# A second place for the attention mask, and other places for three groups of loads and transposes, in a two-layer backbone on one Trainium2 core

## The chip, the core and the metric

The kernel runs on one core of one Trainium2 chip. Five engines work side by side: TensorE (PE) multiplies, VectorE (DVE), ScalarE (ACT) and GpSimd (POOL) do the elementwise work, and SyncE (SP) issues most of the transfers; ACT issues some too. Each engine takes its own instructions in the order written for it and waits on semaphores for the others. The metric is the device time of one execution in microseconds (us), lower being better. The kernel before took 1580.21 us (median of 3 runs, 1580.18 to 1580.25).

## The reference

What is computed is a two-layer generator trunk over 1024 latent tokens and 256 context tokens of width 1024, in fp32:

```
each layer:  x += gate * mixer(adaLN(RMSNorm(x)))
layer 0:     windowed grouped-query attention, 16 heads on 4 key heads, 64 wide,
             window of 128 keys to either side, all context keys, a sink logit
             per head, times silu(gate projection), then the output projection
layer 1:     multi-head latent attention: queries through a latent of 512,
             keys and values through a latent of 256, 32 rotated key columns,
             16 heads, all keys, times silu(gate projection), output projection
end:         RMSNorm of the latent stream
```

The mask of layer 0 says which of the 128-token blocks' keys lie within 128 tokens of a query. The rotation ("rope") multiplies pairs of columns by cosines and sines of the token's row and column.

## The kernel before, in words

**Precision.** An fp32 product is made of three reduced-precision ones. Each operand is split into a high part (line 129, a cast on ACT) and a low part (line 130, a subtraction on DVE or POOL); `mm3` then issues lines 134, 135 and 136 for high times high, low times high and high times low. An operand is ready for the first product when its cast is done, and for the second only when its subtraction is.

**Stages.** Norm and value projection run to about 75 us, and the block-by-block projections of queries, keys and gates to about 323 us. Layer 0's attention then works through 40 units to about 711 us: ten 128-token tiles in the order 2, 0, 3, 1, 4, 5, 6, 7, 8, 9, and four key heads each. A unit has scores for four heads on PE (line 619), the mask, the sink and the row maximum in one DVE pass (line 630), the exponential on ACT (line 633), transposes by 128-key chunk (line 650), the product with the values (lines 667 and 668), and a rescale on POOL. The first tile is special: its keys lie in two 256-wide parts, and each part has a DVE pass of its own. Scores use two pairs of PSUM banks, so the third head's scores need the first head's DVE passes done.

From 711 to about 890 us layer 1 begins. `norm_x` loads a tile of the updated rows (line 233) and scales it (line 235 on ACT for odd tiles). `turn_h` transposes a pair of tiles in four quarters (line 248 on PE, lines 252 and 256 on ACT, 257 on DVE), and `kv_tile` multiplies a tile by the latent key and value weights (24 matmuls 288 wide). Between the tiles lie the first products of the query latent and gate projections. These are done in six groups by Winograd's form of Strassen's scheme, with seven products of sums of quarter matrices for eight. The sums over the tokens are `t_sums` (lines 1146 to 1155). A group's weights are loaded by `fetch` (line 1172), turned into operands by `op`, and multiplied by `P` (12 matmuls of 512 columns each). `early(0)` and `early(1)` fetch and prepare the first two operands of groups 2 and 3 ahead; `first_op` does it for groups 0 and 1. The small fetches (128x4x128) go through rings of 2 KB slots named `wr`. The rest of the query work runs to about 970 us, the latent attention to about 1465 us, and the output projection to the end.

**What sets the order.** Program order and a scheduler set the order on each engine; only the latent attention's loop has an order written by hand. All ordinary loads and stores are issued by SP in a single order, so one that waits for a slot holds back all behind it. `load2` issues on ACT. On-chip memory is laid out by hand in regions (F, R) by offset in KB, so two tensors at one offset share bytes and the later one's load waits for the earlier one's last reader. The mask's bytes in R (offset 92 and up) held projection weights of the last blocks before. The slot at F 4 KB of the early ring lies in the buffer `xr0` (F 4 to 8) from which updated rows are stored. F 0 to 4 is `rows0[0]`, where earlier the cosines of layer 0 (F 0 to 4, until the last key block's rotation) and later those of layer 1 lie.

Of the kernel before, what the change touches and what calls it, by code (L numbers as in the profile page):

```python
# [27 lines left out]
Z = 0.125  # L28
# [32 lines left out]
def kernel(ctx: ExitStack, tc: tile.TileContext, t, out, dbg=None):  # L61
# [480 lines left out]
    mask = r_at(92 + Z, 640).bitcast(F32)  # L542
# [32 lines left out]
    class UnitA:  # L575


        def __init__(self, ti, g):
            self.ti, self.g = ti, g
            self.isx = ti >= 2  # L580
            self.k0, self.k1 = max(2, ti - 1), min(NT - 1, ti + 1)
            self.nloc = (self.k1 - self.k0 + 1) if self.isx else 0
            self.chunks = [0, 1] + (list(range(self.k0, self.k1 + 1)) if self.isx else [])
            self.m = len(self.chunks)
            self.nk = self.m * 128
            self.Ps = []
            self.PT = {}
# [18 lines left out]
        def score(self, h):  # L606
# [20 lines left out]
            for i, (a, b, skip) in enumerate(spans):  # L627
                to = nm if b == self.nk else self.esk[:, h : h + 1]
                mk = mask[:, a + skip : b + skip]
                nc.vector.tensor_tensor_reduce(P[:, a:b], S[:, 256 + a : 256 + b], mk, 1.0, sk, ALU.add, ALU.min, to)  # L630
                sk = to
# [135 lines left out]

    def wkv_copy():
        load(out=wkv_d, in_=w_in1[:, 512:800])

    side = {20: (wkv_copy,), 21: (rows_load, 0), 22: (rows_scale, 0), 31: (rows_load, 1), 33: (rows_scale, 1)}
# [188 lines left out]
    for gp in (1, 2):  # L960
        for bi in (8, 9):
            for c in range(2):
                if (bi, gp, c) == (8, 2, 0):
                    units[0].prep_q()
                    units[0].prep()
                    units[1].prep_q()
                if (bi, gp, c) == (9, 2, 0):
                    units[1].prep()
                    load(out=mask, in_=mask_d)
# [26 lines left out]
    for ui, u in enumerate(units):  # L996
# [11 lines left out]
        for ci in range(u.m):  # L1008
# [15 lines left out]
            next_T()  # L1024
            if ci == u.m - 1:
                if nu is None:
                    xts[1] = shp(xtr.next(), 8, 256)
                    turn_h(1, rows0, xts[1], hT1[1], ada1, range(4))
# [44 lines left out]
    wr = Ring(F, [2, 4], 512)  # L1073
# [59 lines left out]
    def kr_rope():  # L1133
        u = krF[:, 2:10, :]
        o, tmp = [f_at(34.5 + i, 8, 32) for i in range(2)]
# [220 lines left out]
    def first_op(i, n):  # L1356
        groups[i].fetch((n - 1,), 1)
        groups[i].op(n)
# [3 lines left out]
    for i, ti in enumerate(order1):  # L1362
# [9 lines left out]
        if i == 5:  # L1372
            wr = Ring(F, [30, 32, 34], 512)
# [12 lines left out]
        if i == 3:  # L1386
            load(out=cosb, in_=t["cos_b"].rearrange("p (t d) -> p t d", t=8))
            load(out=sinb, in_=t["sin_b"].rearrange("p (t d) -> p t d", t=8))
# [9 lines left out]
        if i in (7, 8):  # L1398
            first_op(0, i - 6)
            first_op(1, i - 6)  # L1400
# [8 lines left out]
    kr_rope()  # L1409
# [9 lines left out]
    for gi, ns in todo:  # L1419
# [5 lines left out]
        for i, n in enumerate(ns):  # L1425
# [6 lines left out]
            if gi == 4 and i in (1, 3):  # L1432
                latent_rms(i)
            if gi == 3 and i == 1:
# [572 lines left out]
```

## Time and profile before

| | |
|---|---|
| median of 3 runs | 1580.21 us |
| profiled execution | 1576.85 us |
| its span (first to last instruction) | 1575.0 us |
| PE busy, 0 to 323 us | 310.6 of 323 |
| PE busy, 323 to 711 us | 378.6 of 388 |
| PE busy, 711 to 784 us | 69.0 of 73 |
| PE busy, 784 to 890 us | 100.3 of 106 |
| PE busy, 890 to 1575 us | 671.3 of 685 |
| mean granted clock of PE | 0.992 of full speed |

The profiled execution lies 1.85 us above its span, and 3.36 us below the median of the runs. A matmul at half clock still counts as busy, so the granted clock has to be read beside the busy time.

### The profile page before, as it was taken

What the parts mean: (1) busy time and instruction counts of PE and PEld (TensorE: products, weight loads), DVE (VectorE), ACT (ScalarE), POOL (GpSimd) and SP (SyncE); (2) the same over time, 40 slices, a digit from 0 to 9 for tenths busy, and PEclk for the clock granted to TensorE, in tenths of its full rate; (3) what the DMA queues carried; (4) which work ended last, traced back from release to release, by engine and by line L of the source; (5) the groups of instructions that cost most, each with busy time, mean ns of one, the idle gap of its engine ahead of it and who ended that gap; (6) DMA issues with size and microseconds to landing.
All of it is one profiled execution on the core that took longest, in us unless ns stands there. A gap on an engine that the chain in (4) does not pass through costs nothing. (4 is left out here: it accounts for less than half of the span.)

```text
span 1575.0 us, 25485 instructions
## 1 busy us (share of the span) xinstructions
PE 1529.6 (97%) x9238; PEld 1147.0 (73%) x9238; DVE 999.6 (63%) x1664; ACT 769.5 (49%) x1477; POOL 779.7 (50%) x816
## 2 busy tenths in 40 slices
PE   6999999989999999998999999999999999999998
PEld 4988888866767777777878878666766766766687
DVE  3969988536555556565765744677577677567354
ACT  4423322257666676665733434555555555555321
POOL 1132212117564445553355252688688688689410
PEclk9999999999999999999999999999999999999999
DMA  9466673554343334324344576223233233244251
GB/s 326 154 198 195 192 212 118 175 165 111 98 124 90 99 91 121 94 81 161 99 132 133 169 242 194 82 72 98 61 98 100 72 91 88 61 138 113 69 168 67
DMA packets 158046, 202.90 MB, mean 129 GB/s; under 512 B 14656, under 2 KB 92480, under 8 KB 157904
## 3 DMA queue, kind: packets, MB, share of 16 engines
q1 hardware_dynamic: 152416, 193.53, 41.5%
q10 hardware_dynamic: 5504, 7.74, 1.4%
q8 instruction: 73, 1.20, 0.3%
q14 instruction: 53, 0.43, 0.1%
HBM read 151.65 MB, written 51.07 MB: 129 GB/s over the span
## 5 line engine op out<-in xcount | busy, mean ns | idle before, releaser
L134 PE MATMUL PB<-arena_r 128*128 128x512 f32 (+2 forms) x990 | 369.8, 376 | 6.5 <-ACT arena_r L129 2.9
L1652 POOL TENSOR_TENSOR arena_f<-arena_f 128x512 f32<-128x512 f32 x252 | 328.0, 1302 | 81.9 <-ACT arena_f L1644 65.0
L135 PE MATMUL PB<-arena_r 128*128 128x512 f32 (+2 forms) x958 | 352.1, 368 | 2.5 <-POOL arena_r L130 2.0
L136 PE MATMUL PB<-arena_r 128*128 128x512 f32 (+2 forms) x926 | 338.5, 366 | 0.1
L130 POOL TENSOR_TENSOR arena_r<-arena_f,arena_r 128x512 fp32r<-128x512 f32 x91 | 128.3, 1422 | 300.9 <-ACT arena_r L129 247.6
L1644 ACT ACTIVATE arena_f<-PB 128x1024 f32<-128x1024 f32 x160 | 164.2, 1027 | 108.5 <-PE PB L1638 69.8
L134 PEld LDWEIGHTS PB<-arena_r 128*128 128x128 f32 x990 | 186.9, 190 | 40.5 <-ACT arena_r L422 4.6
L1603 DVE TENSOR_REDUCE arena_f<-PB 128x1 f32<-128x1024 f32 x128 | 156.0, 1219 | 86.3 <-PE PB L1601 86.2
L135 PEld LDWEIGHTS PB<-arena_r 128*128 128x128 f32 x958 | 181.3, 189 | 30.0 <-POOL arena_r L130 2.6
L136 PEld LDWEIGHTS PB<-arena_r 128*128 128x128 f32 x926 | 175.7, 190 | 28.9 <-issue 1.7
L1638 PE MATMUL PB<-arena_r 64*128 64x512 f32 (+1 forms) x1490 | 194.3, 392 | 0.4 <-ACT arena_f L1644 0.3
L630 DVE CUSTOM_DVE_ANT_0 arena_f<-PB,arena_r,small 128x640 f32<-128x640 f32 (+2 forms) x176 | 124.4, 724 | 85.9 <-PE PB L619 77.2
L1638 PEld LDWEIGHTS PB<-arena_r 64*128 64x128 f32 (+1 forms) x1490 | 135.7, 185 | 29.1 <-ACT arena_f L1644 1.8
L1660 PE MATMUL PB<-arena_f 128*64 128x512 f32 x640 | 144.4, 597 | 0.0
L129 ACT CAST arena_r<-arena_f 128x512 fp32r<-128x512 f32 (+1 forms) x146 | 86.4, 607 | 107.2 <-PE PB L136 24.1
L633 ACT ACTIVATE arena_f<-arena_f,small 128x640 f32<-128x640 f32 (+2 forms) x160 | 118.7, 743 | 37.2 <-DVE small L630 36.3
L619 PE MATMUL PB<-arena_k,arena_r 128*128 128x256 f32 (+1 forms) x576 | 114.5, 321 | 7.5 <-DVE small L630 7.1
L619 PEld LDWEIGHTS PB<-arena_k,arena_r 128*128 128x128 f32 x576 | 82.8, 191 | 36.2 <-issue 14.9
L650 PE MATMUL PB<-ident,arena_f 128*128 128x128 f32 x672 | 104.6, 274 | 1.4 <-ACT arena_f L655 1.1
L1660 PEld LDWEIGHTS PB<-arena_f 128*64 128x64 f32 x640 | 43.1, 136 | 83.2 <-issue 79.6
L199 DVE SCALAR_TENSOR_TENSOR arena_f<-arena_f,small 128x512 f32<-128x512 f32 x126 | 98.4, 829 | 1.0
L136 PE MATMUL PB<-arena_k,arena_r 128*128 128x512 f32 (+2 forms) x274 | 97.8, 357 | 0.0
(249 smaller groups left out, 2513.6 us busy)
## 6 DMA issues: line engine op xcount, KB each, us to landing
arena_f<-ada_w SPq DMA_DIRECT2D x40, 512.0 KB, 4.4
arena_r<-q_d SPq DMA_DIRECT2D x80, 256.0 KB, 4.0
arena_r<-qn_d SPq DMA_DIRECT2D x64, 256.0 KB, 3.8
arena_r<-qr_d SPq DMA_DIRECT2D x170, 64.0 KB, 3.1
arena_f<-a_w_in SPq DMA_DIRECT2D x40, 256.0 KB, 3.1
q_d<-arena_f SPq DMA_DIRECT2D x64, 128.0 KB, 2.4
qn_d<-arena_f SPq DMA_DIRECT2D x16, 512.0 KB, 3.3
arena_f<-b_w_in SPq DMA_DIRECT2D x12, 512.0 KB, 4.0
```

The lines of the kernel that those rows point to most:

```text
L130: (lo_eng or nc.vector).tensor_sub(lo, src, hi.bitcast(F32))
L134: nc.tensor.matmul(o, ah, bh, start=first, stop=False, skip_group_check=more)
L135: nc.tensor.matmul(o, al, bh, start=False, stop=False, skip_group_check=more)
L136: nc.tensor.matmul(o, ah, bl, start=False, stop=last, skip_group_check=more)
L619: nc.tensor.matmul(S[:, at : at + n], qT[:, s, hq, :], kT[:, g, k : k + n], start=s == 0, stop=s == 1)
L630: nc.vector.tensor_tensor_reduce(P[:, a:b], S[:, 256 + a : 256 + b], mk, 1.0, sk, ALU.add, ALU.min, to)
L633: nc.scalar.activation(P, P, AF.Exp, bias=nm, scale=-1.0, accum_out=self.den[:, h : h + 1])
L1603: nc.vector.reduce_max(mx[:, 32 + b : 33 + b], flat, AX.X, negate=True)
L1638: nc.tensor.matmul(S[:, t], k[r, c : c + 128], q[r], start=j == 0, stop=j == 4)
L1644: nc.scalar.activation(E, self.S, AF.Exp)
L1652: eng.tensor_add(self.acc, self.acc, E[:, t])
L1660: nc.tensor.matmul(self.pv[p : p + 64], Vq[:, cs[t], self.h % 4, :], E[:, t], start=i == 0, stop=i == 4)
```

## The change

1. **The mask has two places.** The first, at F 0 KB, is loaded from the input by ACT's queue, during the last projections; the units of the first five tiles (20 units) read it. The second is the old place in R, loaded by SP with unit 4, and read by the other units. The old load, issued just ahead of the first scores, is gone. A copy of weights in memory is moved from unit 20 to unit 19.
2. **The next pair's turns.** `turn_h` for the pair of tiles 2 and 3 was called with the last unit's fourth chunk, all four quarters; now two quarters come with its second chunk and two with its third.
3. **Places of the first query operands.** The early ring of `early(0)` is at F 2 and F 0 instead of F 2 and F 4; the later ring has a fourth slot at F 0. The fetches of the first and second operand of groups 0 and 1 are called one tile earlier than their split, where `first_op` did both.
4. **The rotation of the keys.** The loads of layer 1's cosines and sines and the rotation `kr_rope` move into the loop over the groups, and its scratch to other bytes.

```diff
-    mask = r_at(92 + Z, 640).bitcast(F32)
+    masks = [f_at(0, 640), r_at(92 + Z, 640).bitcast(F32)]
...
+            self.mask = masks[ORDER.index(ti) > 4]
...
-                mk = mask[:, a + skip : b + skip]
+                mk = self.mask[:, a + skip : b + skip]
...
+    def mask_load():
+        load(out=masks[1], in_=mask_d)
...
-    side = {20: (wkv_copy,), 21: (rows_load, 0), ...}
+    side = {4: (mask_load,), 19: (wkv_copy,), 21: (rows_load, 0), ...}
...
                 if (bi, gp, c) == (8, 2, 0):
+                    load2(out=masks[0], in_=t["mask"])
...
                     units[1].prep()
-                    load(out=mask, in_=mask_d)
                     units[2].prep_q()
...
+            if nu is None and 0 < ci < 3:
+                if ci == 1:
+                    xts[1] = shp(xtr.next(), 8, 256)
+                turn_h(1, rows0, xts[1], hT1[1], ada1, (2 * ci - 2, 2 * ci - 1))
             if ci == u.m - 1:
-                if nu is None:
-                    xts[1] = shp(xtr.next(), 8, 256)
-                    turn_h(1, rows0, xts[1], hT1[1], ada1, range(4))
...
-    wr = Ring(F, [2, 4], 512)
+    wr = Ring(F, [2, 0], 512)
...
-        o, tmp = [f_at(34.5 + i, 8, 32) for i in range(2)]
+        o, tmp = [f_at(i, 8, 32) for i in (51, 36)]
...
-            wr = Ring(F, [30, 32, 34], 512)
+            wr = Ring(F, [30, 32, 34, 0], 512)
...
         if i in (7, 8):
-            first_op(0, i - 6)
-            first_op(1, i - 6)
+            for g in groups[0:2]:
+                g.op(i - 6)
+        if i in (6, 7):
+            for g in groups[0:2]:
+                g.fetch((i - 6,), 1)
...
+            if gi == 1 and i == 0:
+                load(out=cosb, ...)
+                load(out=sinb, ...)
+            if gi == 2 and i == 0:
+                kr_rope()
```

How the rows move at three places follows. Line numbers of the changed kernel are up to seven higher; `DMAHW` in a row's waits means a transfer queue's semaphore.

The first place is PE at the start of layer 0's attention, the first unit's scores among products of the last projection (before; four score matmuls make one head of this unit):

```order
L619 MATMUL PB<-arena_k,arena_r 128x256 [waits Activation_49]
L619 MATMUL PB<-arena_k,arena_r 128x256
L134 MATMUL PB<-arena_r 128x512
L619 MATMUL PB<-arena_k,arena_r 128x256 [waits Activation_49]
L619 MATMUL PB<-arena_k,arena_r 128x256
L135 MATMUL PB<-arena_r 128x512
```

and the same place now:

```order
L620 MATMUL PB<-arena_k,arena_r 128x256 [waits Activation_49]
L620 MATMUL PB<-arena_k,arena_r 128x256
L134 MATMUL PB<-arena_r 128x512
L620 MATMUL PB<-arena_k,arena_r 128x256 [waits Activation_49]
L620 MATMUL PB<-arena_k,arena_r 128x256
L620 MATMUL PB<-arena_k,arena_r 128x256 [waits DVE_49]
L620 MATMUL PB<-arena_k,arena_r 128x256
L620 MATMUL PB<-arena_k,arena_r 128x256 [waits DVE_49]
```

The third head's scores, which wait for DVE's pass over the first head, now follow at once; before, six products, the last row of the first list and five behind it, stood ahead of them.

The second place is SP in layer 1's first stage, around the small fetches (L1172), the store of updated rows (L719) and the loads of the next tiles (L233), before:

```order
L701 DMA arena_f<-x 128x1024 [waits DMAHW2_49,Activation_49]
L1172 DMA arena_f<-b_w_in 128x4x128 [waits DMAHW5_49,DMAHW1_49,Pool_49]
L719 DMA x_d<-arena_f 128x1024 [waits DMAHW6_49,DMAHW2_49,DVE_49]
L1172 DMA arena_f<-b_w_in 128x4x128 [waits DMAHW7_49,DMAHW6_49,Activation_49]
L233 DMA arena_f<-x_d 128x1024 [waits DMAHW0_49,PE_49]
```

and now, with the same transfers under lines 702, 1177, 720 and 233, and on to the last small fetch:

```order
L702 DMA arena_f<-x 128x1024 [waits DMAHW5_49,DMAHW1_49,Activation_49]
L1177 DMA arena_f<-b_w_in 128x4x128 [waits DMAHW2_49]
L1177 DMA arena_f<-b_w_in 128x4x128 [waits DMAHW3_49,Pool_49]
L1177 DMA arena_f<-b_w_in 128x4x128 [waits DMAHW6_49,DMAHW2_49,Pool_49]
L720 DMA x_d<-arena_f 128x1024 [waits DMAHW7_49,DMAHW1_49,DVE_49]
L233 DMA arena_f<-x_d 128x1024 [waits DMAHW0_49,PE_49]
L233 DMA arena_f<-x_d 128x1024 [waits PE_49]
L233 DMA arena_f<-x_d 128x1024 [waits DMAHW7_49,DMAHW4_49,PE_49]
L1177 DMA arena_f<-b_w_in 128x4x256 [waits DMAHW6_49,PE_49,Activation_49]
L1177 DMA arena_f<-b_w_in 128x4x256 [waits DMAHW0_49,DVE_49,PE_49]
L1177 DMA arena_f<-b_w_in 128x4x128 [waits DMAHW3_49,DMAHW1_49,Activation_49]
L1437 DMA arena_f<-cos_b 128x256 [waits DMAHW5_49,DMAHW4_49,Pool_49]
```

No small fetch stands between the store and the next tile's load any more. Behind the last row stand the sines (L1438) and then the last small fetch. Six of the eight small fetches now come ahead of the tile's load, five before.

The third place is ACT at the end of the tiles, where the operands of groups 0 and 1 are cast (L129), before:

```order
L129 CAST arena_r<-arena_f 128x512 [waits DVE_49]
L1119 DMA ckv_d<-arena_f 128x256 [waits DMAHW0_49,DVE_49]
L1219 COPY arena_f<-PB 128x512 [waits PE_49]
L129 CAST arena_r<-arena_f 128x512 [waits DVE_49]
L129 CAST arena_r<-arena_f 128x512 [waits PE_49]
L129 CAST arena_r<-arena_f 128x512 [waits DMAHW7_49,Pool_49]
```

and now:

```order
L129 CAST arena_r<-arena_f 128x512 [waits DVE_49]
L1124 DMA ckv_d<-arena_f 128x256 [waits DMAHW1_49,DVE_49]
L1224 COPY arena_f<-PB 128x512 [waits PE_49]
L129 CAST arena_r<-arena_f 128x512 [waits DVE_49]
L129 CAST arena_r<-arena_f 128x512 [waits DMAHW0_49,Pool_49]
L129 CAST arena_r<-arena_f 128x512 [waits DVE_49,PE_49]
```

The cast that waits for a transfer has moved up by one, and the operand that it casts is, going by the rings, another one: before, group 1's first; now, group 0's second.

More of the change, by code (lines that the diff above doesn't have):

```diff
@@ L766, in turn_ctx @@
             split(hT1[0][:, 0, k, :], hT1[0][:, 1, k, :], u)
+    def mask_load():
+        load(out=masks[1], in_=mask_d)
     def wkv_copy():
         load(out=wkv_d, in_=w_in1[:, 512:800])
-    side = {20: (wkv_copy,), 21: (rows_load, 0), 22: (rows_scale, 0), 31: (rows_load, 1), 33: (rows_scale, 1)}
+    side = {4: (mask_load,), 19: (wkv_copy,), 21: (rows_load, 0), 22: (rows_scale, 0), 31: (rows_load, 1), 33: (rows_scale, 1)}
     side.update({23 + 2 * q: (turn_ctx, q) for q in range(4)})
@@ L1354, in early @@
         g.op(2)
-    def first_op(i, n):
-        groups[i].fetch((n - 1,), 1)
-        groups[i].op(n)
     order1 = [2 * p + j for p in (0, 1, 3, 2, 4) for j in range(2)]
@@ L1386 @@
         if i == 3:
-            load(out=cosb, in_=t["cos_b"].rearrange("p (t d) -> p t d", t=8))
-            load(out=sinb, in_=t["sin_b"].rearrange("p (t d) -> p t d", t=8))
             t13 = t_sums(xts[1], xts[3], slice(0, 256), t4buf)
@@ L1408 @@
     next(t24)
-    kr_rope()
     for f in (t13, t24):
@@ L1433 @@
                 latent_rms(i)
+            if gi == 1 and i == 0:
+                load(out=cosb, in_=t["cos_b"].rearrange("p (t d) -> p t d", t=8))
+                load(out=sinb, in_=t["sin_b"].rearrange("p (t d) -> p t d", t=8))
+            if gi == 2 and i == 0:
+                kr_rope()
             if gi == 3 and i == 1:
```

## The prediction

> **What bounds the kernel now.** I read the page's busy shares first, then PE's list of waits, then the stretches around each wait in windows and rows.
>
> ```profile
> PE 1529.6 (97%) x9238; PEld 1147.0 (73%) x9238; DVE 999.6 (63%) x1664; ACT 769.5 (49%) x1477; POOL 779.7 (50%) x816
> ```
>
> PE is busy for 1529.6 of 1575.0 us, so the kernel is PE's work plus 45.4 us of pauses, and only what shortens PE's pauses, or the slow clock behind them, moves the end. Its waits, with columns total, times and longest:
>
> ```profile
> PE PB L619 <- DVE small L630: 7.1, 5, 4.7
> PE PB L248 <- ACT arena_f L235: 3.8, 1, 3.8
> PE PB L134 <- ACT arena_r L129: 3.2, 2, 2.9
> PE PB L1312 <- POOL arena_r L130: 2.2, 1, 2.2
> PE PB L135 <- POOL arena_r L130: 2.0, 1, 2.0
> ```
>
> The first three and the fifth lie where the change works; the fourth lies outside it. Each long one is followed by a stretch at half clock, which PE's busy share hides. I call the three places the mask's, the tile's and the operand's pause.
>
> **The mask's pause.** The cast of the last rotated key block on ACT, SP's load of the mask, DVE's first two passes, PE on either side of the pause, then windows of 2 us (span, PE and its weight loads, DVE, ACT, POOL, granted clock, share and rate of transfers):
>
> ```profile
> 281.65 1.34 ACT L129 CAST arena_k<-arena_f 64x512 fp32r<-64x512 f32 x2 [2.84 <-DVE arena_f L521]
> 322.94 0.54 SPq L969 DMA_DIRECT2D arena_r<-mask_d  x1
> 330.29 0.48 DVE L630 CUSTOM_DVE_ANT_0 arena_f<-PB,arena_r,small 128x256 f32<-128x256 f32 x1 [7.55 <-DMA arena_r<-mask_d]
> 330.70 0.48 DVE L630 CUSTOM_DVE_ANT_0 arena_f<-PB,arena_r,small 128x256 f32<-128x256 f32 x1
> 323.24 0.88 PE L619 MATMUL PB<-arena_k,arena_r 128*128 128x256 f32 x6
> 324.24 0.50 PE L619 MATMUL PB<-arena_k,arena_r 128*128 128x256 f32 x2
> 330.84 0.80 PE L619 MATMUL PB<-arena_k,arena_r 128*128 128x256 f32 x2 [4.72 <-DVE small L630]
> 330.00:332.00 2.00, 1.16 (x4) 1.06 (x5) 1.71 (x9) 0.37 (x1) 0.00 (x0) 0.50 1.09 274
> 332.00:334.00 2.00, 2.00 (x10) 1.81 (x9) 1.39 (x6) 1.24 (x5) 0.00 (x0) 0.50 1.05 212
> 334.00:336.00 2.00, 2.00 (x6) 1.61 (x6) 0.49 (x2) 1.54 (x4) 0.20 (x1) 0.50 0.45 101
> ```
>
> The load goes out when PE has read the last weights in those bytes, shares full transfer engines with the queries' loads, and lands 7 us later. PE stands for 4.72 us and then runs 1.16 + 2 + 2 = 5.16 us of busy time at half clock, which is 2.6 us of lost time. Together: 7.3 us.
>
> The change loads this mask on ACT's queue, just ahead of the cast at 281.65, some 40 us earlier, so DVE's passes can start with the first scores at 323.24. One ACT issue is added there; ACT has idle time on both sides, so I cost it at nothing. What comes next is DVE's own pace. Passes start 0.41 us apart (330.29, 330.70), and the third head's scores, now right behind the second's, need the first head's two passes. With the first pass at about 323.8 these are done by 324.6, while PE arrives at 324.24 + 0.3. I leave 0.5 us for this and count **6.8**. Bounds: 7.3 if DVE keeps up, and 4.0 if PE waits for the first unit's eight passes one by one (8 × 0.41 = 3.3). The second mask's load has a whole run of units to land in, and costs PE nothing.
>
> **The tile's pause.** SP, POOL, ACT and PE around it, then windows:
>
> ```profile
> 737.97 0.45 SPq L719 DMA_DIRECT2D x_d<-arena_f  x1
> 742.30 0.37 SPq L1172 DMA_DIRECT2D arena_f<-b_w_in  x1
> 742.76 0.46 SPq L233 DMA_DIRECT2D arena_f<-x_d  x1
> 732.80 4.68 POOL L130 TENSOR_TENSOR arena_r<-arena_f,arena_r 128x512 fp32r<-128x512 f32 x3 [6.14 <-PE PB L135]
> 745.40 0.62 ACT L129 CAST arena_r<-arena_f 128x512 fp32r<-128x512 f32 x1 [3.46 <-DMA arena_f<-b_w_in]
> 746.89 1.14 ACT L235 ACTIVATE arena_f<-arena_f,small 128x1024 f32<-128x1024 f32 x1
> 748.09 0.66 PE L248 MATMUL PB<-ident,arena_f 128*128 128x128 f32 x4 [3.79 <-ACT arena_f L235]
> 748.00:750.00 2.00, 1.91 (x12) 1.92 (x13) 1.56 (x2) 1.77 (x3) 1.52 (x1) 0.77 0.00 0
> 750.00:752.00 2.00, 2.00 (x10) 2.00 (x9) 2.00 (x3) 1.43 (x5) 0.00 (x0) 0.50 0.19 66
> 752.00:754.00 2.00, 2.00 (x15) 2.00 (x15) 1.56 (x5) 1.92 (x5) 0.99 (x1) 0.88 0.01 4
> ```
>
> The small fetch at 742.30 goes into bytes from which the store at 737.97 still reads; SP stands for it, and the tile's load goes out only behind it, at 742.76. The price is 3.8 us of pause and a clock loss of 1.91 × 0.23 + 2 × 0.50 + 2 × 0.12 = 1.7 us: 5.5 us.
>
> With the ring at F 2 and F 0 that fetch no longer waits for the store, and all early fetches stand ahead of it. One more fetch now waits for a POOL subtraction. The three of 732.80 take 1.56 us each, so a fourth ends at 737.48 + 1.56 = 739.0, and the load goes out after the store's issue, at about 739.5. From issue to line 235 took 746.89 − 742.76 = 4.1, giving 743.6. ACT's own wait began at 745.40 − 3.46 = 741.9; the work behind it, up to line 235, took 1.5 us, and a cast of the token sums of about 1 us comes in front, so ACT is free at about 744.3, and line 235's 1.14 us end at 745.4. PE stopped at 748.09 − 3.79 = 744.3 and has three products more in front, 744.7 by my reckoning, so 0.7 us are left. I count **4.8**. Bounds: 5.5, and 2.0 if the store's own wait, for DVE, holds the load to 741.5 (1.3 us earlier than before, with 0.7 us of the clock loss).
>
> **The operand's pause.** PE, the ACT cast and the POOL subtraction that end the two waits (each the third of four in a row), and windows:
>
> ```profile
> 787.23 0.79 PE L134 MATMUL PB<-arena_r 128*128 128x512 f32 x1 [2.88 <-ACT arena_r L129]
> 790.07 0.80 PE L135 MATMUL PB<-arena_r 128*128 128x512 f32 x1 [2.05 <-POOL arena_r L130]
> 793.80 0.40 PE L135 MATMUL PB<-arena_r 128*128 128x512 f32 x1
> 796.55 0.39 PE L135 MATMUL PB<-arena_r 128*128 128x512 f32 x1
> 786.56 0.62 ACT L129 CAST arena_r<-arena_f 128x512 fp32r<-128x512 f32 x1
> 788.75 1.27 POOL L130 TENSOR_TENSOR arena_r<-arena_f,arena_r 128x512 fp32r<-128x512 f32 x1
> 786.00:788.00 2.00, 0.77 (x1) 0.29 (x1) 0.44 (x1) 2.00 (x5) 1.78 (x2) 0.66 0.73 186
> 790.00:792.00 2.00, 1.93 (x5) 1.55 (x6) 2.00 (x4) 0.55 (x2) 1.71 (x2) 0.50 0.00 0
> 792.00:794.00 2.00, 2.00 (x7) 1.62 (x6) 1.75 (x5) 0.00 (x0) 1.25 (x2) 0.64 0.00 0
> ```
>
> The pauses are 2.88 + 2.05 = 4.9 us, and the clock costs 0.77 × 0.34 + 1.93 × 0.50 + 2 × 0.36 = 1.95: 6.9 us. The product that waits is group 1's first. Its operand would now be fetched with the early ones, at about 740, and be split long before. But the third cast and the third subtraction of that row of four are still there, now for group 0's second operand, which PE needs one product later. Twelve matmuls last 796.55 − 793.80 = 2.75 us. So the cast, done at 787.2, meets PE at 787.1 and costs nothing, while the subtraction, done at 790.0, meets a need at 787.3: a wait of 2.7 us stays. What such a wait does to the clock shows outside the change, behind the fourth line of the list:
>
> ```profile
> 920.00:925.00 5.00, 5.00 (x19) 3.94 (x18) 3.56 (x9) 2.71 (x5) 4.40 (x5) 0.68 0.98 278
> ```
>
> After that 2.2 us wait, 5 us ran at 0.68, a loss of 1.6. So 2.7 + 1.6 = 4.3 stays of 6.9, and I count **2.6**. Bounds: 6.9 if the operand comes early enough, and a loss of 1 if the two loads of cosines and sines, now ahead of the last small fetch, delay it by their 0.9 us of issue (0.46 each, as at 742.76).
>
> The Trainium skill (TensorE: Matmul & The Clock Gate, "HAM oscillation — how this bites in real kernels") puts the limit for a pause without harm to the clock at about 3.4 us. By that rule the 1.6 us would not be lost, and the sum would be 1.6 larger. The trace differs: a pause of 2.2 us was followed by a clock of 0.68.
>
> **The turns of the next pair.** PE at the end of layer 0 beside an undisturbed pair of the same product:
>
> ```profile
> 705.79 0.60 PE L667 MATMUL PB<-arena_v 128*64 128x512 f32 x2
> 711.30 1.07 PE L667 MATMUL PB<-arena_v 128*64 128x512 f32 x2
> 714.49 1.07 PE L667 MATMUL PB<-arena_f,arena_v 128*64 128x512 f32 x2
> ```
>
> Between the quarters of the turn, two pairs take 1.07 us instead of 0.60, waiting for ACT's evacuation of the transposes. Spread among the output projection's products, the 16 transposes let ACT catch up: 2 × 0.47 = **0.9**. Bounds: 1.0, and a loss of 0.8 if one quarter waits for a bank.
>
> The rest is moved work. The largest operation of the key rotation:
>
> ```profile
> 790.49 1.50 DVE L1136 TENSOR_TENSOR arena_f<-krF,arena_f 128x256 f32<-128x256 f32 x1
> ```
>
> The rotation is only moved within DVE's work of the same groups, which PE waits for in none of the five lines; two activation-table loads fewer fall on ACT, off PE's path. Both count nothing; uncovered, the rotation would cost PE that 1.5 us.
>
> **Sum.** 6.8 + 4.8 + 2.6 + 0.9 = 15.1. From the profiled 1576.85 that gives 1561.75. The median of the runs lies 3.36 higher, so 1580.21 − 15.1 = **1565.1 us**. All lower bounds together gain 4.2 (1576.0), all upper ones 20.7 (1559.5).
>
> **Rivals.**
> - *The operand's pause goes wholly.* For it: seven of the eight fetches are out before the last one's place. Against: the four casts stand in the same place of ACT's queue, behind DVE's sums. 4.3 more: 1560.8.
> - *The 2.7 us wait leaves the clock alone*; it is under 3 us long. The 920 us window speaks against. 1.6 more: 1563.5. This is where the rule of the Trainium skill's page TensorE: Matmul & The Clock Gate would put the time.
> - *The pause moves.* Only the mask's part comes in full; the tile's load is held by the store's wait (2.0), and the last fetch comes later (−1). 6.8 + 2.0 − 1 + 0.9 = 8.7: 1571.5. For it: the fetches still go through one queue in front of the tile.
> - *Nothing to be seen.* The first mask's bytes come free later than I read, or the load lands no earlier. Against: the last reader of those bytes is done by the last key rotation, some 40 us ahead.
> - *Slower.* The cosines' load waits on a POOL subtraction and blocks SP. If that is the fourth of the row, done at 790.0 + 1.3 = 791.3, the last small fetch goes out at 792.2, lands 3.1 later (742.30 to 745.40), and after cast and subtraction (0.6 + 1.3) is ready at 797.2, 10.1 us after PE's need at 787.1. The large fetch behind it comes as late and costs 10.1 − 2.75 = 7.4 more; with two clock losses of 2.6, as behind the mask, the place costs 22.7 instead of 6.9, and the kernel loses 15.8 − 12.5 = 3.3: 1583.5. It decides from a wait of the cosines' load beyond 791; the three single subtractions that stand ahead of the row of four speak against it.
>
> **Chances.** Forecast (1562 to 1568) 0.55; pause wholly gone 0.14; clock unharmed 0.08; pause moved 0.15; nothing 0.04; slower 0.04. Within 0.2% (3.2 us), which is what a measurement of this kernel can tell from no change, lies the fifth case. So faster 0.92, same 0.04, slower 0.04. The range runs from the wholly gone pause, 1560, past the moved one, to 1574.
>
> **What would show it.** Right: no wait of PE on line 630's pass over 1 us and full clock from 330 to 336; the tile's load ahead of 740 (less what the mask's part has moved), and under 1 us in front of its transposes; one wait of about 2.7 us on a subtraction at the end of the tiles, with a dip of the clock behind it. Wrong: a new wait of PE on line 633 or 650 in the first units, SP standing in front of the cosines, or the casts of the last four coming apart.

## The result, and the profile after

The changed kernel takes **1566.58 us** (median of 6 runs, 1564.85 to 1569.09) beside 1579.62 for the kernel before on the same chip (6 runs, 1577.72 to 1580.25). The ratio is 0.9918, with a 95% interval of 0.9906 to 0.9931. That is 13.0 us less, where 15.1 were forecast. The profiled execution took 1564.85 us, with a span of 1563.1.

The busy shares and PE's list of waits, after:

```profile
PE 1525.8 (98%) x9238; PEld 1146.3 (73%) x9238; DVE 1002.6 (64%) x1664; ACT 765.7 (49%) x1475; POOL 780.5 (50%) x816
PE PB L1317 <- POOL arena_r L130: 4.7, 2, 2.4
PE PB L135 <- POOL arena_r L130: 2.7, 1, 2.7
PE PB L248 <- ACT arena_f L235: 1.9, 1, 1.9
PE PB L620 <- DVE small L631: 1.7, 3, 1.1
PE PB L248 <- ACT arena_f L252: 1.3, 1, 1.3
```

Of the three pauses the mask's is gone (7.1 us on the scores' line before, 1.7 now; the longest one left, 1.06 us in a later unit, stood there before as well with 1.08), the tile's is two smaller ones (3.8 before; 1.9 and 1.3), and of the operand's the second wait alone is left (2.9 and 2.0 before; 2.7). The first line of the list, two waits of 2.30 and 2.36 us behind 900 us, lies outside the change; the same two transposes waited 2.18 and 0.81 us in the first profile of the kernel before, 1.93 and 2.12 in its second.

**The mask's place.** ACT's load, SP's second load, PE's scores and DVE's first passes, then windows:

```profile
282.88 0.36 ACTq L968 DMA_DIRECT2D arena_f<-mask  x1
335.33 0.42 SPq L770 DMA_DIRECT2D arena_r<-mask_d  x1
325.18 0.88 PE L620 MATMUL PB<-arena_k,arena_r 128*128 128x256 f32 x6
326.18 0.97 PE L620 MATMUL PB<-arena_k,arena_r 128*128 128x256 f32 x6
325.62 0.48 DVE L631 CUSTOM_DVE_ANT_0 arena_f<-PB,arena_f,small 128x256 f32<-128x256 f32 x1 [0.80 <-PE PB L620]
326.10 0.48 DVE L631 CUSTOM_DVE_ANT_0 arena_f<-PB,arena_f,small 128x256 f32<-128x256 f32 x1
330.00:332.00 2.00, 2.00 (x10) 1.69 (x9) 0.00 (x0) 0.48 (x3) 1.22 (x2) 1.00 1.09 331
332.00:334.00 2.00, 2.00 (x10) 1.65 (x9) 0.00 (x0) 1.05 (x1) 0.00 (x0) 1.00 1.05 209
334.00:336.00 2.00, 2.00 (x11) 1.65 (x10) 0.00 (x0) 1.99 (x4) 0.00 (x0) 1.00 1.05 226
```

DVE's first pass starts 0.44 us after the scores; PE has neither a pause nor a slow stretch there.

**The tile's place.** POOL, SP, DVE, ACT and PE, then windows:

```profile
726.14 6.38 POOL L130 TENSOR_TENSOR arena_r<-arena_f,arena_r 128x512 fp32r<-128x512 f32 x4 [7.88 <-ACT arena_r L129]
733.02 0.76 SPq L720 DMA_DIRECT2D x_d<-arena_f  x1
733.88 1.18 SPq L233 DMA_DIRECT2D arena_f<-x_d  x2
731.30 2.31 DVE L1151 TENSOR_TENSOR arena_f<-arena_f 128x1024 f32<-128x1024 f32 x1
735.83 0.56 ACT L252 ACTIVATE arena_f<-PB,small 128x256 f32<-128x256 f32 x1 [2.25 <-DVE arena_f L1123]
739.88 1.15 ACT L235 ACTIVATE arena_f<-arena_f,small 128x1024 f32<-128x1024 f32 x1 [1.57 <-DMA arena_f<-x_d]
736.45 0.44 PE L248 MATMUL PB<-ident,arena_f 128*128 128x128 f32 x2 [1.26 <-ACT arena_f L252]
741.08 0.66 PE L248 MATMUL PB<-ident,arena_f 128*128 128x128 f32 x4 [1.94 <-ACT arena_f L235]
735.00:740.00 5.00, 2.88 (x21) 2.47 (x19) 4.04 (x6) 2.60 (x7) 0.47 (x1) 1.00 0.91 303
740.00:745.00 5.00, 3.92 (x20) 3.92 (x21) 3.74 (x5) 3.85 (x9) 0.07 (x1) 0.70 0.12 42
```

The store of updated rows (L720) and two tile loads (L233) of 0.5 MB each go out within 2 us, and the transfer engines are 0.91 busy. The first of these loads lands 6.0 us after its issue (739.88 − 733.88); before, line 235 began 4.1 us after it, with the second load behind it as well, but with the store 4.8 us ahead instead of 0.9. A new wait of 1.26 us stands in front: PE waits for an evacuation of ACT (L252), ACT for a pass of DVE (L1123) behind which a store of the latent keys and values stands in ACT's queue, and DVE had been held by a token sum of 2.31 us while POOL worked on its four subtractions.

**The operand's place.** POOL's four subtractions in a row, PE, and windows:

```profile
777.64 6.94 POOL L130 TENSOR_TENSOR arena_r<-arena_f,arena_r 128x512 fp32r<-128x512 f32 x4 [2.10 <-ACT arena_r L129]
782.41 0.50 PE L135 MATMUL PB<-arena_r 128*128 128x512 f32 x1 [2.75 <-POOL arena_r L130]
780.00:785.00 5.00, 2.58 (x7) 2.13 (x8) 5.00 (x4) 3.04 (x7) 5.00 (x4) 0.80 0.57 176
785.00:790.00 5.00, 5.00 (x20) 4.01 (x20) 4.52 (x9) 2.58 (x5) 1.68 (x3) 0.86 0.21 79
```

One wait is left, of 2.75 us, with 2.58 × 0.20 + 5 × 0.14 = 1.2 us of slow clock in these windows.

### Where the 13 us came from, by stage

The profiles of all kernels of this study share the same PE work in each stage, so a stage's length can be compared between them. Lengths are read from PE's rows: layer 0 from the first scores to the last product with the values, the tiles from there to the last of the 288-wide products, the operand's place from there to the first product of a token sum (three products of 12 matmuls, group 1's first among them), and the rest from there to the end of the span.

| kernel | start | layer 0 | tiles | operand's place | rest |
|---|---|---|---|---|---|
| before | 323.2 | 392.3 | 68.8 | 15.4 | 775.3 |
| before, second profile | 325.2 | 390.5 | 68.9 | 16.5 | 775.9 |
| mask's part alone | 325.3 | 383.6 | 69.0 | 16.6 | 775.4 |
| all but the mask's part | 325.3 | 391.0 | 66.2 | 13.1 | 773.7 |
| rotation's part alone | 325.3 | 392.1 | 68.8 | 15.5 | 775.1 |
| after | 325.2 | 383.7 | 67.7 | 12.8 | 773.7 |
| after, second profile | 325.8 | 384.5 | 66.5 | 14.2 | 775.2 |

Layer 0 is 391.5 on the mean with the old mask (four profiles) and 383.9 with the new (three): 7.5 less. The six other profiles with the new mask lie at 383.4 to 386.4 (three of them, 384.6, 385.1 and 386.4, have no edit in layer 0 beside it); with all nine the mean is 384.5, and the gain 7.0. The tiles fall from 68.9 (four) to 66.8 (three): 2.1. The operand's place falls from 16.0 to 13.4: 2.6. The rest falls from 775.4 to 774.2: 1.2. The sum, 13.4, is the 13.0 of the medians within the spread of single profiles, which is up to 1.8 us in a stage of this table and 3.0 in layer 0 of those nine.

The start differs too, though nothing is changed ahead of it; the first experiment below shows that it belongs to the execution.

### The profile page after: what moved, and what is told of

Read it like the earlier page. It is cut to its first block, busy times and chain, and to the rows that moved or that the text cites. A ratio compares the mean times of both kernels' runs of the same rounds, so it can differ in the third digit from the quotient of the medians.

```text
span 1563.1 us, 25489 instructions
## 1 busy us (share of the span) xinstructions
PE 1525.8 (98%) x9238; PEld 1146.3 (73%) x9238; DVE 1002.6 (64%) x1664; ACT 765.7 (49%) x1475; POOL 780.5 (50%) x816
## 4 chain that ended last, share of the span: by engine, by line
PE 78%; POOL 7%; issue 6%; ACT 3%; DVE 3%; DMA 3%; SPq 0%; POOLq 0%; DVEq 0%; ACTq 0%
PE PB L134 13%; PE PB L135 13%; PE PB L136 13%; PE PB L1645 12%; PE PB L1667 9%; PE PB L1608 4%; PE PB L668 3%; PE PB L620 3%; PE PB L651 2%; POOL small L644 1%; POOL arena_r L130 1%; PE PB L1616 1%; POOL arena_f L719 1%; PE PB L1696 1%; POOL arena_f L692 1%
## 5 line engine op out<-in xcount | busy, mean ns | idle before, releaser
L129 ACT CAST arena_r<-arena_f 128x512 fp32r<-128x512 f32 (+1 forms) x146 | 86.7, 607 | 110.8 <-PE PB L136 28.7
L620 PEld LDWEIGHTS PB<-arena_k,arena_r 128*128 128x128 f32 x576 | 81.3, 189 | 30.8 <-issue 16.5
L651 PEld LDWEIGHTS PB<-ident,arena_f 128*128 128x128 f32 x672 | 81.4, 140 | 18.8 <-ACT arena_f L634 7.2
```

The lines of the kernel that those rows point to most:

```text
L620: nc.tensor.matmul(S[:, at : at + n], qT[:, s, hq, :], kT[:, g, k : k + n], start=s == 0, stop=s == 1)
L651: nc.tensor.transpose(pt[:, h, :], self.Ps[h][:, ci * 128 : ci * 128 + 128], ident)
```

## The experiments

All ratios are against the kernel before on the same chip.

### The kernel before, a second profile

No edit.

> The kernel before once more, for a second profile of it. In the profile of before the clock stood at 1.00 from 35 to 45 us; in the four profiles taken since of changed kernels it fell to about 0.55 and 0.78 there, although nothing is changed in that stage. Theory: this stretch differs by execution, not by kernel, so this profile may show the slow stretch; if it does, the first scores come at about 325.2 instead of 323.2, and the pause in front of the mask is about 3.7 instead of 4.72 us, so that the mask's part is worth 1 us less in such an execution. Rival: the slow stretch comes with the change, and this profile shows 1.00 in 35 to 45 us and first scores at 323.2.

Measured: 1578.77 us in one run, span 1577.0. Windows and scores of this profile of the kernel before:

```profile
35.00:40.00 5.00, 3.85 (x17) 3.56 (x18) 3.62 (x9) 4.44 (x11) 1.10 (x2) 0.50 1.03 368
40.00:45.00 5.00, 5.00 (x36) 4.85 (x36) 3.12 (x10) 3.28 (x7) 1.37 (x2) 0.82 0.56 201
325.19 0.88 PE L619 MATMUL PB<-arena_k,arena_r 128*128 128x256 f32 x6
331.55 0.50 PE L619 MATMUL PB<-arena_k,arena_r 128*128 128x256 f32 x2 [3.46 <-DVE small L630]
```

The theory holds: the slow stretch at 35 to 45 us (0.50 and 0.82) comes with the unchanged kernel as well, the scores start 2.0 us later, and the mask's pause is 3.46 instead of 4.72 us. So the profile from which the prediction was worked out was of an execution without that stretch, and its layer 0 was 1.8 us longer than this one's (392.3 against 390.5). Against this profile the new mask is worth 6.6 (390.5 − 383.9), against the first one 8.4. That the start makes this difference is not shown: with the same slow start and the old mask, the kernel with the rotation's part alone waits 4.1 us for the mask and takes 392.1 in layer 0, and all but the mask's part 3.7 us and 391.0.

### The mask's part alone

The kernel before with all of part 1:

```diff
+    masks = [f_at(0, 640), r_at(92 + Z, 640).bitcast(F32)]
...
+                    load2(out=masks[0], in_=t["mask"])
-                    load(out=mask, in_=mask_d)
```

> The kernel before with the mask's two places alone (part 1). Reading of the changed kernel's trace: between the first scores and the middle of layer 0's attention it gained 8.4 us, more than the 6.8 forecast. If that is the mask's doing alone, this kernel gains 7.5 to 8.5 us, a time of about 1571.5, with the tile's pause (3.8) and the operand's pauses (2.9 and 2.0) as before. Rival: part of it came from the other parts through a different order; then this kernel gains under 6.8, 1573 or more.

Measured: 1572.0 us (1571.75 to 1573.68), ratio 0.9954 (0.9939 to 0.9969): 7.1 us less than before. In the table its layer 0 is as short as in the changed kernel, and its tiles and its operand's place are as long as before. The mask's part works by itself. The gain lies 0.4 below the 7.5 to 8.5 expected from one pair of profiles, and above the rival's 6.8.

### All but the mask's part

The changed kernel with all of part 1 undone:

```diff
-    masks = [f_at(0, 640), r_at(92 + Z, 640).bitcast(F32)]
+    mask = r_at(92 + Z, 640).bitcast(F32)
...
-                    load2(out=masks[0], in_=t["mask"])
+                    load(out=mask, in_=mask_d)
```

> The changed kernel with the old mask load (parts 2, 3 and 4 without part 1). If the parts are independent, its gain and that of the mask alone add to the 13.0 us of the whole: about 5 us here, 1574.6, with PE's pause of about 4.7 us on the mask back. Rival: the parts help each other (the place at F 0 is shared by mask, ring and cosines), and the two gains miss 13.0 by over 2 us.

Measured: 1572.04 us (1571.16 to 1574.33), ratio 0.9954 (0.994 to 0.9969): 7.1 us less. The two halves give 14.2 together, the whole change 13.0; the difference of 1.2 is within the intervals, so nothing speaks for an interaction. The time is 2.6 us less than the 1574.6 expected, which was worked out from a mask worth 8.4; the pause in front of the mask is back, with 3.7 us.

### Without the earlier fetches

The changed kernel with these lines:

```diff
+    def first_op(i, n):
+        groups[i].fetch((n - 1,), 1)
+        groups[i].op(n)
-            wr = Ring(F, [30, 32, 34, 0], 512)
+            wr = Ring(F, [30, 32, 34], 512)
-            for g in groups[0:2]:
-                g.op(i - 6)
-        if i in (6, 7):
-            for g in groups[0:2]:
-                g.fetch((i - 6,), 1)
+            first_op(0, i - 6)
+            first_op(1, i - 6)
```

> The changed kernel, but the fetches of the first two operands of groups 0 and 1 come with their split again, and the later ring has three slots; the early ring at F 2 and F 0 and all other parts stay. Nothing is left out of the computation. Theory: the operand's part of the change is in these fetches alone. Its two pauses of 2.9 and 2.0 us come back with their slow clock, 2.6 us more than the changed kernel, 1569.2, and the pauses in front of the tile's transposes stay as they are now (1.3 and 1.9). Rival: the early ring alone makes the difference, since the fetch that waited is ahead in the queue anyway; then the time stays at 1566.6. Second rival: the added fetches are what holds up the tile's load in the changed kernel; then the pauses of 1.3 and 1.9 go, and the time is 1567 with the operand's pauses back.

Measured: 1570.42 us (1565.61 to 1571.61), ratio 0.9927 (0.9899 to 0.9954); the median does not tell 2.6 us here, the profile does:

```profile
738.29 0.44 PE L248 MATMUL PB<-ident,arena_f 128*128 128x128 f32 x2 [1.27 <-ACT arena_f L252]
781.78 0.79 PE L134 MATMUL PB<-arena_r 128*128 128x512 f32 x1 [2.84 <-ACT arena_r L129]
784.87 0.80 PE L135 MATMUL PB<-arena_r 128*128 128x512 f32 x1 [2.30 <-POOL arena_r L130]
```

Both waits of the operand's place are back, and that stage is 15.3 us long, as before. The tile's waits stay (1.27 here, and 2.42 on line 235). So the operand's gain is in the earlier fetches (with their fourth slot), and these are not what holds up the tile's load.

### Without the turns' part

The changed kernel with these lines:

```diff
-            if nu is None and 0 < ci < 3:
-                if ci == 1:
-                    xts[1] = shp(xtr.next(), 8, 256)
-                turn_h(1, rows0, xts[1], hT1[1], ada1, (2 * ci - 2, 2 * ci - 1))
             if ci == u.m - 1:
+                if nu is None:
+                    xts[1] = shp(xtr.next(), 8, 256)
+                    turn_h(1, rows0, xts[1], hT1[1], ada1, range(4))
```

> The changed kernel with the second part undone: all four quarters of the next pair's turn come with the last unit's fourth chunk again. Nothing is left out of the computation. Forecast of the prediction: 0.9 us slower than the changed kernel, 1567.5 where that has 1566.6. What the two traces say: nothing is lost or gained (the lead over the kernel before was 6.6 us on either side of this place), so the same time, 1566.6, and a layer 1 that begins at 708.8 as in the changed kernel. A loss of over 1.5 us would refute both.

Measured: 1569.06 us (1565.32 to 1570.69), ratio 0.9922 (0.9899 to 0.9945). At the place itself nothing changes. The rows are a pair of transposes of the last unit, ahead of the turns, and the last products with the values; first the kernel before (its last products stand in the prediction at 714.49), then the changed kernel:

```profile
708.28 0.41 PE L687 MATMUL PB<-ident,arena_f 128*128 128x128 f32 x2
```

```profile
701.65 0.41 PE L688 MATMUL PB<-ident,arena_f 128*128 128x128 f32 x2
706.97 1.93 PE L668 MATMUL PB<-arena_f,arena_v 128*64 128x512 f32 x6
```

From 708.28 to 714.49 + 1.07 are 7.28 us before; from 701.65 to 706.97 + 1.93 are 7.25 us after; without the part, 7.30. But the profile without the part has longer tiles, 69.2 us, with 3.45 us in front of the odd tile's transposes:

```profile
730.68 3.31 SPq L1176 DMA_DIRECT2D arena_f<-b_w_in  x2
734.10 0.87 SPq L720 DMA_DIRECT2D x_d<-arena_f  x1
735.06 1.14 SPq L233 DMA_DIRECT2D arena_f<-x_d  x2
743.67 1.12 PE L248 MATMUL PB<-ident,arena_f 128*128 128x128 f32 x4 [3.45 <-ACT arena_f L235]
```

The order on SP is that of the changed kernel there, where the two small fetches go out at 729.60 and 732.55, the store at 733.02 and the load at 733.88, with nearly the same spacing. Only the load lands later, 7.4 us after its issue instead of 6.0; in the two other profiles with this order and spacing (the changed kernel's second, and all but the mask's part) line 235 began 5.4 and 5.2 us after it. So one order of issues goes with 5.2 to 7.4 us, and what decides within that is open. The median lies 2.5 us above the expected 1566.6, beyond the 1.5 that was to refute both readings; the ratios on the same chips, 0.9922 and 0.9918, differ by far less than their intervals. So the runs do not tell whether the part is worth the 1.5 to 2.7 us that the single profiles' tiles differ by.

### The rotation's part alone

The kernel before with part 4:

```diff
-            load(out=cosb, ...)
-            load(out=sinb, ...)
-    kr_rope()
+            if gi == 1 and i == 0:
+                load(out=cosb, ...)
+                load(out=sinb, ...)
+            if gi == 2 and i == 0:
+                kr_rope()
```

> The kernel before with the fourth part alone: the loads of the cosines and sines and the rotation of the keys in the loop over the groups. Nothing is left out of the computation. Forecast of the prediction: no change, 1579.5 to 1580.5. What the traces of before and after say: about 1.3 us are gained between the last of group 1's first products and the end of the groups, where two waits of PE on sums of DVE (0.2 and 0.6) are gone; if these come from the rotation's place, the time is about 1.3 us less than before. Rival: the rotation now stands in front of those sums in the queue of DVE and costs its 1.5 us there.

Measured: 1579.35 us (1576.73 to 1581.16, 10 runs), ratio 1.0001 (0.9992 to 1.001). No change, as the prediction had it. The 1.2 us that the rest of the kernel is shorter do not come from this part by itself. The traces show where most of them come from. From the end of the operand's place to the first transposes of the list's L1312 (L1317 in the changed kernel), PE took 106.1 us without a wait in the four profiles with parts 3 and 4 as they are (after, its second profile, all but the mask's part, without the turns' part). It took 106.9 to 107.5 before (two profiles), with the mask's part alone and with the rotation's part alone, and 107.1 without the earlier fetches; there PE waits 0.2 to 0.7 us on sums of DVE or a cast of ACT. So 0.8 to 1.4 us need the earlier fetches. What differs behind that, in the two waits past 900 us, differs as much between profiles of one kernel.

### The early low parts on DVE

The changed kernel; in `early`, the low parts of the second operands of groups 2 and 3 are made by DVE:

```diff
-        g.op(2)
+        g.A12 = g.put(g.raw(0, 1), nc.vector)
```

> The changed kernel with the low parts of the second early operands of groups 2 and 3 made by DVE instead of POOL. In the changed kernel PE still waits 1.3 us (for the last quarter of a turn) and 1.9 us (for the scaled tile) here. Theory: both come from the fourth subtraction in a row on POOL. It holds the small fetch that stands ahead of the tile's load (732.55, load at 733.88) and it holds POOL's rms power, through which DVE, then ACT's store of the latent, then ACT's evacuation of the turn are late. With two passes fewer the load goes out about 3 us earlier, both waits and the dip of the clock go: 4 to 4.8 us gained, 1562. Rival: the tile's load is late because it shares the transfer engines with what goes out just ahead of it (it took 6.0 us to land against 4.1 before), then only the 1.3 us go and the time is 1565 or more.

Measured: 1566.99 us (1565.23 to 1568.39), ratio 0.9922 (0.9906 to 0.9939): no gain over the changed kernel. The waits of 1.26 and 1.94 us are gone, and so is the slow clock behind them. In their place PE waits 0.64 us for ACT there, 1.43 us for a copy of ACT at 767, and these two:

```profile
732.40 0.40 PE L134 MATMUL PB<-arena_k,arena_r 128*128 128x288 f32 x1 [2.02 <-DVE arena_f L718]
783.12 0.50 PE L135 MATMUL PB<-arena_r 128*128 128x512 f32 x1 [1.81 <-POOL arena_r L130]
```

The theory was right that both waits go with the subtractions, and wrong that the time goes with them: the tiles take 67.8 us, as in the changed kernel's first profile. The rival's time came, but not its reason, since the wait on the load went as well; the load went out 3.1 us behind the store here, and line 235 began 4.0 us after it.

### The later ring in another order

The changed kernel with:

```diff
-            wr = Ring(F, [30, 32, 34, 0], 512)
+            wr = Ring(F, [32, 30, 34, 0], 512)
```

> The changed kernel with the first two slots of the later ring swapped (F 32, 30, 34, 0 instead of 30, 32, 34, 0), so that group 0's second operand goes to F 32 and group 1's to F 30, whose bytes a store of group 3's gate still reads. Theory: the 2.75 us pause at the end of the tiles is there because group 0's second operand is fetched late, behind that store, and so comes third among four POOL subtractions; in a slot that nobody reads it is ready early, and group 1's, needed 2.75 us later, takes the third place: the wait falls to under 0.6 us, the dip of the clock goes, 3.5 to 4.3 us gained, 1562.5. Rival: POOL's four passes as such set the pace, the wait moves by one product and stays about as long: 1565.5 to 1567.

Measured: 1565.57 us (1564.87 to 1566.12), ratio 0.9911 (0.9896 to 0.9926). The wait of 2.75 us is gone, and two others have come, 1.36 us on a copy of ACT and the one below. In front of the tile's transposes the 1.26 us are there again, but only 0.26 on line 235, although POOL's four subtractions stay. Neither the theory nor the rival foresaw this: the wait went as the theory has it, and the time stayed in the rival's range because work of ACT and DVE came late in its place. The new wait and the window behind it:

```profile
796.92 0.50 PE L134 MATMUL PB<-arena_r 128*128 128x512 f32 x1 [2.19 <-DVE arena_f L1236]
795.00:800.00 5.00, 3.08 (x14) 2.55 (x14) 2.96 (x5) 0.63 (x1) 1.59 (x1) 1.00 0.45 85
```

### Three edits, and four

The changed kernel with the three edits of the first diff, and then also with that of the second:

```diff
-    side = {..., 33: (rows_scale, 1)}
+    side = {..., 35: (rows_scale, 1)}
-        g.op(2)
+        g.A12 = g.put(g.raw(0, 1), (nc.vector, nc.gpsimd)[i])
-            wr = Ring(F, [30, 32, 34, 0], 512)
+            wr = Ring(F, [32, 30, 34, 0], 512)
```

```diff
-                nc.vector.tensor_sub(s3, raw(0, 0), raw(1, 0))
+                (nc.gpsimd if self.c0 == 800 else nc.vector).tensor_sub(s3, raw(0, 0), raw(1, 0))
```

> The changed kernel with three edits at the pauses that are left: the low part of one of the two early second operands is made by DVE instead of GpSimd; the later ring of four slots is used in the order 32, 30, 34, 0; the scaling of the second tile of updated rows stands with unit 35 instead of 33. Nothing is left out of the computation. Theory: what is left is single late operands. The pause of 1.3 us in front of the tile's transposes goes, its load goes out 1.5 us earlier and the pause of 1.9 shrinks below 1; the pause of 2.75 us on a subtraction goes with its slow clock (1.3). Together about 4 us: 1562.5. Rival: the same work is only late on another engine. DVE and ACT are as full there as GpSimd, new pauses of 1 to 2 us come on a copy, a cast or a sum of DVE, as they did where each edit was made alone (gains of 0 and 1 us), and the time stays at 1565 to 1566.6.

Three edits measured: 1565.25 us (1563.45 to 1566.08), ratio 0.9901 (0.9883 to 0.9919), 2.7 us short of the theory, and not told apart from the changed kernel by its interval. The tiles are 64.9 us and the operand's place 9.4, 2.8 and 3.4 less than in the changed kernel's first profile. But 5.0 of these 6.2 are lost in the rest (778.7 against 773.7). Most of it is one wait on a sum of DVE, behind a subtraction for group 2 that stood in front of it in DVE's queue and waited for its weights, and the slow clock after that wait:

```profile
790.85 1.45 DVE L1202 TENSOR_TENSOR arena_f<-arena_f 128x512 f32<-128x512 f32 x1 [1.50 <-DMA arena_f<-b_w_in]
793.75 0.50 PE L134 MATMUL PB<-arena_r 128*128 128x512 f32 x1 [2.40 <-DVE arena_f L1236]
795.00:800.00 5.00, 5.00 (x16) 3.95 (x15) 1.38 (x3) 1.24 (x2) 0.00 (x0) 0.66 0.62 157
```

The fourth edit moves that subtraction to POOL:

> The last experiment's three edits, and a fourth: one subtraction for group 2, which stood in front of group 0's sums in the queue of DVE and waited there 1.5 us for its weights, is made by GpSimd. Nothing is left out of the computation. Theory: the pause of 2.4 us on that sum and the slow clock behind it (5 us at 0.66, 1.7) go, 4 us less than with three edits, and the kernel takes about 1561.5, 4 to 5 us less than the changed kernel beside it. Rival: GpSimd now waits for the same weights, the low part behind it is 1.5 us late, and PE waits for that instead; then the time stays at 1565.

Measured: **1562.45 us** (1560.44 to 1564.55), ratio 0.9891 (0.9878 to 0.9905). Beside it on the same chip ran the changed kernel again:

> The changed kernel once more, beside the kernel with four edits on the same chip. Expected 1566.6 and, in the profile, the three pauses of the first one: 1.3 and 1.9 us in front of the tile's transposes, 2.75 us on the subtraction. If a pause is gone or another has come, it belongs to the execution and not to the kernel.

Measured: 1567.86 us (1566.16 to 1570.14), ratio 0.9925 (0.9912 to 0.9937), with the same three pauses (1.27, 1.68 and 2.75 us). The two intervals do not overlap: the kernel with four edits is 5.4 us faster than the changed kernel by the medians. What the fourth edit alone adds to the three is not told by the intervals, which overlap; the profiles show its wait and the slow clock gone, and the rest of the kernel 776.4 us long where it was 778.7. Its sum now comes early, and the window that ran at 0.66 runs at full clock:

```profile
789.30 0.69 DVE L1236 TENSOR_TENSOR arena_f<-PB,arena_f 128x512 f32<-128x512 f32 x1
795.00:800.00 5.00, 5.00 (x24) 4.14 (x23) 3.40 (x5) 2.20 (x4) 1.29 (x1) 1.00 0.34 68
```

## Why the prediction was right, and where not

The forecast of 1565.1 us lies 1.5 below the measured 1566.58, and the four terms of its sum did not come out alike. The gain is 2.1 short (13.0 of 15.1); the median of the kernel before was 0.6 lower beside the changed kernel than when the forecast was made, and 1.2 us gained outside every term made up for part of the shortfall. That the time came this close is in so far luck.

- **The mask, 6.8.** Right in mechanism, and in size as far as it can be told. The mask's part alone measured 7.1, and layer 0 is 6.6 to 8.4 shorter, by which profiles are compared (7.0 to 7.5 on the means); the upper bound of 7.3 was read from a single profile. DVE's pace, for which 0.5 was left, costs nothing that the rows show.
- **The tile, 4.8.** The way was right, the size was not: 2.1 on the mean of three profiles, 1.1 in the first one. The step that failed is "the load goes out ... at about 739.5", with 4.1 us to line 235. Less the 6.66 us by which layer 1 starts earlier, 739.5 is 732.8; the load went out at 733.88, 1.0 later, and took 6.0 us, 1.9 longer. So 1.94 us stay where 0.7 were left. The 4.1 us had been read with the store 4.8 us ahead; with the store 0.9 us ahead the transfer engines are 0.91 busy. That this is what slows the load is argued and not shown; for it speaks that the load was quicker (4.0) where the store stood 3.1 us ahead.

  The fourth subtraction on POOL, which the prediction counted as a delay of the fetch alone, goes with a late DVE (2.31 us for a sum of tokens) and through it a late evacuation of ACT: 1.26 us in front of the transposes that no term had. With 1.2 us of slow clock in 740 to 745 (3.92 × 0.30), 4.4 of the 5.5 us are there again. That the 1.26 us are POOL's is borne out: the wait stands at 1.25 to 1.27 us in all six profiles of kernels with part 3 and four subtractions in a row, and in none of the three with fewer, of which one differs from the changed kernel in that alone. The wait on line 235 is less settled: 0.26 to 3.45 us in those six, and the landing of the load behind it varies as said above. With both away (three and four edits) the tiles take 64.9 and 65.0 us, 3.9 less than before, so most of the 4.8 was there to be had. Of the signs that the prediction named, those of the mask and the operand came (but for the old wait of 1.06 us in a later unit) and those of the tile did not.
- **The operand, 2.6.** Right in size and in mechanism: 2.6 by the stages, with one wait of 2.75 us on a subtraction (2.7 forecast) and a slow clock behind it (1.2, forecast 1.6). Undoing the fetches brought both waits back. The 0.8 to 1.4 us further on that need these fetches stood in no term.
- **The turns, 0.9.** Nothing: 7.28 us before, 7.25 after. The step that failed is "two pairs take 1.07 us instead of 0.60, waiting for ACT". Two rows of 0.64 and 0.59 us that start 0.47 us apart show that two matmuls one behind the other take 1.06 us without any wait. The row of 0.60 us was of two that run side by side, going by its length and by line 667, which puts the outputs of even and odd chunks in different halves of the partitions. Rows of the kernel before:

```profile
704.46 0.64 PE L667 MATMUL PB<-arena_v 128*64 128x512 f32 x1
704.93 0.59 PE L667 MATMUL PB<-arena_f,arena_v 128*64 128x512 f32 x1
```

- **The rotation and the table loads, 0.** Right for the rotation (1.0001).
- **The 3.36 us between the profile and the median.** About 2 of them are the slow stretch at the start, which the first profile did not have and 11 of the 13 profiles have. Subtracting the sum from the median is right as far as the terms do not depend on that stretch. With the old mask, layer 0 took 392.3 us without it and 390.5 to 392.1 with it, so no dependence is shown.

Of the rivals, the wait that leaves the clock unharmed fell in this place: the windows after 2.75 us ran at 0.80 and 0.86. The wholly gone pause did not come, but shows up at once when the ring's order is changed. The pause moved in part, as the third rival had it for the tile (2.0, measured 2.1), while its loss at the operand did not come. The cosines' load went out at 766.1, far ahead of the row of four subtractions (777.64), so the slower case did not arise.

## What to carry to other kernels

When a late operand is brought forward, the engine that now makes it early is loaded at another place: count what stands behind the added instructions on that engine, and on the engine that waits for it, before the gain is booked. Once several engines are nearly full at one place, edits made alone give little (0 and 1 us here), because the next late operand is only 1 to 2 us behind; three together gave no gain clear of the noise, and four gave 5.4. A profile is one execution: a stage that no edit touches and that differs between two profiles says how far the read sizes can be trusted.

## What the runs showed of the hardware

- **The start varies.** Of 13 profiles, 11 have a clock of 0.50 to 0.95 in windows between 35 and 45 us, around three pauses of 0.5 to 1.1 us; the first profile of the kernel before and the one with four edits have 1.00. It moves all that follows by about 2 us (first scores at 323.2 and 323.6 against 324.9 to 326.1). The first two pauses, 0.54 and 0.5 us, are the same with and without it. In six profiles the stretch begins ahead of the third: the two matmuls behind the second pause last 0.63 to 0.80 us instead of 0.50. The third pause and the window, first of the kernel before, then of the changed kernel:

```profile
36.93 0.66 PE L411 MATMUL PB<-ident,arena_f 128*128 128x128 f32 x4 [1.13 <-DVE arena_r L423]
35.00:40.00 5.00, 3.57 (x29) 3.37 (x30) 4.06 (x11) 4.90 (x11) 1.10 (x2) 1.00 1.03 383
```

```profile
36.90 1.11 PE L411 MATMUL PB<-ident,arena_f 128*128 128x128 f32 x4 [1.00 <-DVE arena_r L423]
35.00:40.00 5.00, 3.73 (x17) 3.44 (x18) 3.62 (x9) 4.44 (x11) 1.10 (x2) 0.55 1.04 387
```

  The Trainium skill (TensorE: Matmul & The Clock Gate, "What's actually happening") says that the gate judges PE's activity in a window that runs freely beside the kernel. The profiles agree with that but do not prove it: the same pauses stand at the same place, and the clock falls ahead of the third, behind it, or not at all.
- **No length of pause decides alone.** The same wait on the same sum of DVE was followed by full clock after 2.19 us and by 0.66 after 2.40 (the rows above); 1.94 us behind 1.26 gave 0.70. The Trainium skill (TensorE: Matmul & The Clock Gate, "HAM oscillation — how this bites in real kernels") warns of gaps above about 3.4 us; here the clock fell after shorter ones.
- **A sum of DVE takes longer beside POOL's subtractions.** The token sum took 2.31 us in all six profiles where it starts beside the last of four subtractions, and 1.21 or 1.22 in the seven where they were over. With three edits they end at 731.09, and the sum takes:

```profile
731.63 1.21 DVE L1151 TENSOR_TENSOR arena_f<-arena_f 128x1024 f32<-128x1024 f32 x1
```
